# Every fourth chunk of the feed-forward weights: the remainder formed by an accumulating transfer instead of VectorE

## The chip, the cores and the metric

The kernel runs on one core of a Trainium2 chip. The metric is the device time of one execution, in microseconds, as the median of several runs; before the change it is 1503.18 us (three runs, 1502.87 to 1503.75).

## The reference, cut to what matters

One decoder layer over 256 tokens of width 2048, all in float32: a gated token mixer of two attention branches, a cross-attention into 256 memory tokens, and a SwiGLU feed-forward part. The change touches only the last:

```
def swiglu(x, w_in, w_out):
    g, u = jnp.split(x @ w_in, 2, axis=-1)
    return (jax.nn.silu(g) * u) @ w_out

    y = swiglu(x, w_ffn_in[l], w_ffn_out[l])
    x = layer_norm(ALPHA * x + y, ln_g[l, 2], ln_b[l, 2])
```

`w_ffn_in` is 2048 x 11264 (two halves of 5632 columns), `w_ffn_out` is 5632 x 2048.

## The kernel before

Every large product is [256 tokens, K] times streamed weights [K, 512]. TensorE takes float32 operands in its rounded form `F32R`, so each operand is split in two: hi is the value rounded to `F32R`, lo = value - hi is what the rounding leaves. A product then takes three matmuls for each block of 128 rows of K: hi x hi, hi x lo and lo x hi.

The weights come in chunks of 256 rows of K (two blocks, `KC = 2`) by 512 columns, 512 KB each. `chunk_in` (L193) brings one in:

- a load issued on SyncE's queue puts it into a tile `raw` (L204; pool of 5 buffers),
- ScalarE writes hi, the first half of a tile `hl`, by a copy that rounds (L116; pool of 4 buffers),
- VectorE writes lo = raw - hi into the second half (L117).

`chunk_mm` (L214) then issues six matmuls for each of the two groups of 128 tokens: L221 reads hi, L222 reads lo, L223 reads hi, twice over. That is 12 matmuls a chunk, into two accumulators of PSUM. `product` (L225) runs over the chunks. The feed-forward part (L816 on) has 11 column blocks of `w_ffn_in`, each with a gate product and an up product of 8 chunks, and then 4 column blocks of `w_ffn_out` with 22 chunks each. The first gate product and the last output product keep their last 8 chunks on chip (`seq=8`).

Nothing orders the engines but semaphores: a `hl` buffer is written again when the matmuls of the chunk four before have read it; a `raw` buffer is loaded again when its last reader is done; and SyncE's queue is in order, so a load that waits for its buffer holds back every transfer behind it. The order of the instructions on each engine is set when the kernel is built. Beside the chunks, SyncE also moves the finished blocks of the hidden activations out (`spill`, L190) and back in turned order (`turn`, L176).

Of the kernel before, what the change touches and what calls it, by code (L numbers as in the profile page):

```python
# [12 lines left out]
AF = mybir.ActivationFunctionType  # L13
ALU = mybir.AluOpType
# [14 lines left out]
DFF = 5632  # L29
# [8 lines left out]
KC = 2  # L38
NTURN = 2
W = 512  # L40


class Side:
    """Work that is emitted in small steps between the chunks of the main products."""

    def __init__(self):
        self.queue = []
# [18 lines left out]
def trunk(ctx: ExitStack, tc: tile.TileContext, a, out: bass.AP):  # L66
    nc = tc.nc
# [8 lines left out]
    last = [None]  # L76
    later = []
# [25 lines left out]
    def f(ap):  # L103
        return ap.bitcast(F32)

    class Quad:
        """Four blocks [128, 256] and what their rounding leaves, as operands of products."""

        def __init__(self, k=4, t=256):
            self.t = b8()  # L110
# [5 lines left out]
        nc.scalar.activation(hi, src, AF.Copy)  # L116
        (eng or nc.vector).tensor_tensor(lo, src, f(hi), op=ALU.subtract)  # L117

    # ---- constants
    ident = const.tile([P, P], F32, name="ident")  # L120
    make_identity(nc, ident)
    identr = const.tile([P, P], F32R, name="identr")
# [4 lines left out]
    for tt in range(NT):  # L127
        k = P * (tt + 1)
# [16 lines left out]
        return t  # L145

    def rstd(dst, var, scale):
        """(var * scale + eps) ** -0.5"""
        nc.gpsimd.tensor_scalar(dst, var, scale, EPS, op0=ALU.mult, op1=ALU.add)
        nc.gpsimd.tensor_tensor(dst, dst, mhalf, op=ALU.pow)  # L150

    # ---- transposes of [128 tokens, 512] into a quad
    def to_quad(q, tt, src):
        p = ps_aux()
        for i in range(4):
# [6 lines left out]
        to_quad(q, tt, src)  # L162
        yield

    # ---- the same for 256 tokens, from DRAM: the loads put columns 128 a .. 128 a + 127 into partitions
    # 32 a .. 32 a + 31, so that transposes of 32 by 32 are all that is left. Partition p of block k holds
    # column 4 p + k (mixed), or column 32 k + p % 32 of those (not mixed).
    def turn(q, src, mixed=True):
        q.mixed = mixed
        yield from turned(q.hi, q.lo, src, mixed)  # L170
# [18 lines left out]
    def keep(d, tt, src):  # L189
        nc.sync.dma_start(d[tt * P:(tt + 1) * P, :], src)  # L190

    # ---- products with streamed weights: [256 tokens, kts * 128] @ [kts * 128, n]
    def chunk_in(pieces, c, n, held=False, mixed=False, fine=None, eng=None):  # L193
        raw = stream.tile([P, KC, W], F32, tag="raw", name=nm("raw"), bufs=5)
        at = 0
        for w in pieces:
            m = w.shape[1]
            if mixed:
                g = c * KC // 4
                rows = w[g * W:(g + 1) * W, :].rearrange("(p k) n -> p k n", k=4)[:, c * KC % 4:c * KC % 4 + KC, :]  # L200
            else:
                rows = w[c * KC * P:(c + 1) * KC * P, :].rearrange("(k p) n -> p k n", p=P)
            for k in ([slice(i, i + 1) for i in range(KC)] if fine else [slice(0, KC)]):
                last[0] = nc.sync.dma_start(raw[:, k, at:at + m], rows[:, k, :])  # L204
                if fine:
                    next(fine, None)
            at += m
        t = b8() if held else stream.tile([P, D], F32R, tag="hl", name=nm("hl"), bufs=4)
        hi, lo = [t[:, i * KC * W:(i + 1) * KC * W].rearrange("p (k n) -> p k n", k=KC) for i in range(2)]
        for k in ([slice(i, i + 1) for i in range(KC)] if fine else [slice(0, KC)]):  # L210
            split(hi[:, k, :n], lo[:, k, :n], raw[:, k, :n], eng)
        return hi, lo
# [9 lines left out]
            nc.tensor.matmul(o[:, :n], xh, lo[:, kk, :n], start=False, stop=False)  # L222
            nc.tensor.matmul(o[:, :n], xl, hi[:, kk, :n], start=False, stop=k == kts - 1)  # L223

    def product(act, pieces, steps=1, before=None, first=None, seq=0, stream_seq=0, done=None):  # L225
        """act: quads; pieces: DRAM views of the weights' columns. The last seq chunks of weights stay on
        chip, and the first 128 tokens go through them before the others do."""
        n = sum(w.shape[1] for w in pieces)
        kts = pieces[0].shape[0] // P
        nchunk = kts // KC  # L230
        out = [ps_acc() for _ in range(NT)]
        for c in range(nchunk - seq):
            w = chunk_in(pieces, c, n, mixed=act[c * KC // 4].mixed, fine=first if c == 0 else None)
            if first is not None and c == 0:
                for _ in first:
                    pass
            if before is not None:
                before(c)
            for tt in range(NT):
                chunk_mm(out[tt], act, tt, c, kts, n, w)  # L240
            flush()
            side.step(steps)
        if seq:
            ws = []
            for i, c in enumerate(range(nchunk - seq, nchunk)):
                ws.append(chunk_in(pieces, c, n, held=i >= stream_seq, mixed=act[c * KC // 4].mixed, eng=nc.gpsimd if i % 4 == 2 else None))
                chunk_mm(out[0], act, 0, c, kts, n, ws[-1])
                side.step(steps)
            done(0, out[0])
            for i, c in enumerate(range(nchunk - seq, nchunk)):  # L250
                chunk_mm(out[1], act, 1, c, kts, n, ws[i])
                side.step(steps)
            done(1, out[1])
        elif done is not None:
            for tt in range(NT):
                done(tt, out[tt])
        return out
# [3 lines left out]
        nc.tensor.matmul(o, lh, rl, start=False, stop=False)  # L261
        nc.tensor.matmul(o, ll, rh, start=False, stop=stop)  # L262

    # ---- inputs
    x, mem = a["x"][0], a["mem"][0]
    w_in = a["w_in"][0]

# [15 lines left out]
    x0 = first_x()  # L283
    next(x0)

    # ---- the weights of the latents
    ukT, uv = [], []

    def latent_weights():
# [22 lines left out]
            uv.append(q)  # L312
            yield

    # ---- indexer queries: [hi; lo] of a head on the partitions
    qi = []
    for g in range(2):
        if g == 1:
# [3 lines left out]
        for tt in range(NT):  # L322
# [4 lines left out]
            for i in range(2):  # L327
                p = ps_aux(F32R)
# [4 lines left out]
                nc.scalar.activation(t[:, i * 4:i * 4 + 4, sl], pt, AF.Copy)  # L333
        qi.append(t)

    # ---- indexer keys, latents
    kvg = row_of(a["kv_norm_g"][0], LAT, "kvg")
    kig = row_of(a["idx_k_norm_g"][0], IDIM, "kig")
    kib = row_of(a["idx_k_norm_b"][0], IDIM, "kib")
# [7 lines left out]
    for tt in range(NT):  # L347
        sl = slice(tt * P, (tt + 1) * P)
        p = ps[tt]
# [29 lines left out]
            nc.tensor.transpose(pc[:, cc * P:(cc + 1) * P], ckv[tt].rearrange("p (c k) -> p k c", k=2)[:, cc], ident)  # L379
        split(ckT[:, 0, :, sl], ckT[:, 1, :, sl], pc[:, :2 * P].rearrange("p (c t) -> p c t", c=2))  # L380

    # ---- keys and values of the heads from the latents
    khT, vh = [], []

    def latent_heads():
# [43 lines left out]
            later.append(turn(q, d, False))  # L429
        return q  # L430

    # ---- attention of four heads
    def attention(q, kT, v, bias, slopes, oT, causal):
        width = 384 if causal else 512
        PT = [b8()[:, :4 * width].rearrange("p (h t) -> p h t", h=4) for _ in range(2)]
# [143 lines left out]
    side.finish()  # L579
    side.add(dsa())  # L580

    # ---- gate of the first branch, before its sigmoid
    ma = [b8(F32) for _ in range(NT)]
    for j in range(4):
        bias = bias_chunk(a["b_gate"][0][0, j * W:(j + 1) * W])
# [1 line left out]
        for tt in range(NT):  # L587
            nc.vector.tensor_tensor(ma[tt][:, j * W:(j + 1) * W], ps[tt], bias, op=ALU.add)

    # ---- block attention: one block, so causal over all keys  # L590
    oTb = [None, None]

    def moba(g, q, k, v):
# [10 lines left out]
    for g in range(2):  # L604
# [3 lines left out]
        side.add(moba(g, qm, km, vm))  # L608
        if g == 0:
            pass  # L610
    # the first branch must be done
    while oTa[1] is None or any(gen.__name__ == "dsa" for gen in side.queue):
        side.step(1)
    for tt in range(NT):
# [30 lines left out]
        q.mixed = True  # L645
        mT.append(q)

    # ---- residual and layer norm
    tok = []

    def load_row(dst, src):
# [10 lines left out]
            yield from load_row(tok[tt], x[tt * P:(tt + 1) * P, :])  # L662

    class Norm:
        """Residual sums and the layer norm over them."""

        def __init__(self, i):
            self.i = i
# [29 lines left out]
            eng.tensor_tensor(t, t, self.rows[1][:, cs], op=ALU.add)  # L698

        def run(self, tts, lag, far=()):  # L700
            """Blocks of 512 columns: norm, then transposes some steps later; those in far through DRAM."""
            if self.quads is None:
                self.quads = [Quad() for _ in range(4)]
            sc = {tt: self.scales(tt) for tt in tts}
            todo = [(tt, j) for j in range(4) for tt in tts]
            spills = {j: spill() for j in far}
            for i in range(len(todo) + lag):
                if i < len(todo):
                    tt, j = todo[i]
                    self.block(tt, j, sc[tt])  # L710
                    if j in far:
                        keep(spills[j], tt, tok[tt][:, j * W:(j + 1) * W])
                if i >= lag:
                    tt, j = todo[i - lag]
                    if j not in far:
                        to_quad(self.quads[j], tt, tok[tt][:, j * W:(j + 1) * W])
                    elif tt == tts[-1]:
                        for _ in turn(self.quads[j], spills[j]):
                            yield
                yield  # L720
# [46 lines left out]
            side.add(load_mem())  # L767
    side.finish()

    # ---- cross-attention  # L770
    w_kv = a["w_kv_mem"][0]
    side.add(n1.run(range(NT), 6, (2, 3)))
    side.step(2)
# [28 lines left out]
    for tt in range(NT):  # L802
        for j in range(4):
            p = ps_acc()
            kts = NMH * HD // P
# [6 lines left out]
        side.step(1)  # L812
    x2T = n2.quads

    # ---- feed-forward
    hT = []  # L816
    wf = a["w_ffn_in"][0]
    for j in range(DFF // W):
        gs = []

        def gate(tt, p):
            g = stage()
            nc.scalar.activation(g, p, AF.Silu)
            gs.append(g)

        if j == 0:
            product(x2T, [wf[:, j * W:(j + 1) * W]], seq=8, stream_seq=3, done=gate)
            side.finish()
        else:
            product(x2T, [wf[:, j * W:(j + 1) * W]], done=gate)  # L830
        pu = product(x2T, [wf[:, DFF + j * W:DFF + (j + 1) * W]])
        q = Quad()
        d = spill()
        for tt in range(NT):
            nc.vector.tensor_tensor(gs[tt], gs[tt], pu[tt], op=ALU.mult)
            keep(d, tt, gs[tt])
        later.append(turn(q, d))
        q.mixed = True
        hT.append(q)
    n3 = Norm(2)  # L840
    side.add(n3.load())
    for j in range(4):
        def finish(tt, p):
            n3.add(tt, j, p)
            if j == 3:
                n3.finish(tt)

        product(hT, [a["w_ffn_out"][0][:, j * W:(j + 1) * W]], seq=8 if j == 3 else 0, stream_seq=3, done=finish)


_INS = ["x", "mem", "w_in", "b_gate", "kv_norm_g", "idx_k_norm_g", "idx_k_norm_b", "w_uk", "w_uv", "w_o_dsa",
# [21 lines left out]
```

## Time and profile before

| what | value |
|---|---|
| median of three runs | 1503.18 us |
| span of the profiled execution | 1506.3 us, 3.1 us above the median |
| TensorE busy | 1464.6 us, 97% of the span |
| VectorE busy | 929.2 us, 62% |
| ScalarE busy | 684.2 us, 45% |
| GpSimd busy | 55.6 us, 4% |
| mean busy share of the 16 DMA engines on SyncE's queue | 69.7% |

No time of the profiled execution other than its span is given, so the span stands for it. How to read it: matmuls are pipelined, so a row of 0.39 us for one matmul overlaps the next; the distance between two starts is what one costs. An engine's busy share says nothing of who waits for whom; the rows that do are those of the waits, and those of the timeline, which give a start, a duration, and in brackets the idle time before it and what ended it.

### The profile page before, as it was taken

To read this page: it belongs to the slowest core of one execution; us is meant where nothing else is said; L and a number is where in the kernel's file an instruction comes from. 1 tells how busy PE (TensorE), PEld (TensorE's weight loads), DVE (VectorE), ACT (ScalarE), POOL (GpSimd) and SP (SyncE) were. 2 spreads that over 40 slices of the span, in tenths; PEclk is the share of its full clock that TensorE was granted. 3 is DMA by queue.
4 is the path that set the end of the run, shared out by engine and by line. 5 is a ranking of instruction groups with operands and counts; after the bars stand their busy time and mean duration, and the time that the engine had idled before them with its cause. 6 is when DMAs were issued, how large, how long until landed. Compare 5 with 4: busy or idle time off the path is not lost.

```text
span 1506.3 us, 17772 instructions
## 1 busy us (share of the span) xinstructions
PE 1464.6 (97%) x6640; PEld 1214.9 (81%) x6640; DVE 929.2 (62%) x1145; ACT 684.2 (45%) x798; POOL 55.6 (4%) x63
## 2 busy tenths in 40 slices
PE   7999999999999999889989999999999999999996
PEld 5988888888888887677878888888888888888885
DVE  6666986575756665776784555555455455545455
ACT  4645456454444443354753444444344444333342
POOL 0010000000000000040030000000000000000003
PEclk9999999999999999899999999999999999999998
DMA  9966667777667789749636667776777777666662
GB/s 272 235 181 185 193 207 233 220 251 224 206 200 224 230 257 281 192 141 298 204 117 201 208 210 222 222 220 204 231 217 204 223 219 248 193 200 190 194 218 88
DMA packets 201623, 318.71 MB, mean 212 GB/s; under 512 B 18880, under 2 KB 60992, under 8 KB 201536
## 3 DMA queue, kind: packets, MB, share of 16 engines
q1 hardware_dynamic: 201536, 317.57, 69.7%
q8 instruction: 52, 0.85, 0.2%
q14 instruction: 35, 0.29, 0.1%
HBM read 299.70 MB, written 17.83 MB: 211 GB/s over the span
## 4 chain that ended last, share of the span: by engine, by line
PE 51%; DVE 3%; DMA 1%; ACT 1%; issue 1%; POOL 0%; SPq 0%; ACTq 0%; DVEq 0%
PE acc L222 17%; PE acc L223 17%; PE acc L221 17%; DVE b L696 1%; DMA raw<-in_w_kv_mem 1%; DVE b L739 1%; PE aux L156 0%; ACT b L116 0%; DVE b L117 0%; DVE b L698 0%; DVE b L741 0%; DVE hl L117 0%; DVE lnst L681 0%; DVE b L680 0%; PE aux L261 0%
## 5 line engine op out<-in xcount | busy, mean ns | idle before, releaser
L117 DVE TENSOR_TENSOR hl<-raw,hl 128x1024 fp32r<-128x1024 f32 (+2 forms) x493 | 595.8, 1217 | 414.2 <-ACT hl L116 413.0
L116 ACT ACTIVATE hl<-raw 128x1024 fp32r<-128x1024 f32 (+2 forms) x495 | 516.2, 1051 | 592.4 <-PE acc L223 537.3
L222 PE MATMUL acc<-hl,b 128*128 128x512 f32 (+1 forms) x1976 | 771.8, 391 | 13.7 <-DVE hl L117 13.7
L221 PE MATMUL acc<-hl,b 128*128 128x512 f32 (+1 forms) x1976 | 769.5, 391 | 2.4 <-ACT b L182 1.7
L223 PE MATMUL acc<-hl,b 128*128 128x512 f32 (+1 forms) x1976 | 769.7, 390 | 1.1 <-DVE b L184 0.9
L222 PEld LDWEIGHTS acc<-hl,b 128*128 128x128 f32 x1976 | 373.3, 189 | 91.6 <-DVE hl L117 16.6
L221 PEld LDWEIGHTS acc<-hl,b 128*128 128x128 f32 x1976 | 373.3, 189 | 79.2 <-ACT b L182 2.5
L223 PEld LDWEIGHTS acc<-hl,b 128*128 128x128 f32 x1976 | 373.2, 189 | 78.8 <-DVE b L184 2.4
L181 DVE STREAM_TRANSPOSE tr<-turn 128x256 f32<-128x256 f32 (+1 forms) x156 | 71.3, 515 | 105.7 <-DMA turn<-spill 84.5
L182 ACT ACTIVATE b<-tr 128x1024 fp32r<-128x1024 f32 (+1 forms) x39 | 39.5, 1016 | 123.0 <-DVE tr L181 119.6
L184 DVE TENSOR_TENSOR b<-tr,b 128x1024 fp32r<-128x1024 f32 (+1 forms) x39 | 45.3, 1167 | 3.6 <-ACT b L182 3.0
L116 ACT ACTIVATE b<-aux 128x512 fp32r<-128x512 f32 (+1 forms) x44 | 23.2, 538 | 29.3 <-PE aux L262 15.5
L117 DVE TENSOR_TENSOR b<-aux,b 128x512 fp32r<-128x512 f32 (+1 forms) x44 | 26.1, 610 | 11.9 <-ACT b L116 11.7
L117 POOL TENSOR_TENSOR hl<-raw,hl 128x1024 fp32r<-128x1024 f32 x2 | 5.6, 2802 | 718.7 <-ACT hl L116 718.7
L222 PE MATMUL acc<-b,b 128*128 128x512 f32 x72 | 28.0, 391 | 0.3 <-DVE b L117 0.3
L221 PE MATMUL acc<-b,b 128*128 128x512 f32 x72 | 28.0, 393 | 0.1
L223 PE MATMUL acc<-b,b 128*128 128x512 f32 x72 | 27.9, 389 | 0.0
L117 DVE TENSOR_TENSOR b<-raw,b 128x1024 fp32r<-128x1024 f32 x16 | 23.1, 1461 | 7.7 <-ACT b L116 7.7
L261 PE MATMUL aux<-b,b 128*128 128x256 f32 (+1 forms) x80 | 21.9, 282 | 0.0
L116 ACT ACTIVATE b<-raw 128x1024 fp32r<-128x1024 f32 x18 | 18.4, 1059 | 5.9 <-DMA raw<-in_w_ffn_out 5.4
L262 PE MATMUL aux<-b,b 128*128 128x256 f32 (+1 forms) x80 | 21.0, 279 | 0.0
L260 PE MATMUL aux<-b,b 128*128 128x256 f32 (+1 forms) x80 | 20.8, 274 | 0.0
(129 smaller groups left out, 531.8 us busy)
## 6 DMA issues: line engine op xcount, KB each, us to landing
raw<-in_w_ffn_in SPq DMA_DIRECT2D x176, 512.0 KB, 4.5
raw<-in_w_in SPq DMA_DIRECT2D x143, 512.0 KB, 4.2
raw<-in_w_ffn_out SPq DMA_DIRECT2D x88, 512.0 KB, 4.2
raw<-in_w_out SPq DMA_DIRECT2D x32, 512.0 KB, 5.6
spill<-stage SPq DMA_DIRECT2D x56, 256.0 KB, 4.1
turn<-spill SPq DMA_DIRECT2D x112, 128.0 KB, 3.1
raw<-in_w_o_dsa SPq DMA_DIRECT2D x16, 512.0 KB, 4.5
raw<-in_w_o_moba SPq DMA_DIRECT2D x16, 512.0 KB, 4.2
```

The costliest lines, as they stand in the source:

```text
L116: nc.scalar.activation(hi, src, AF.Copy)
L117: (eng or nc.vector).tensor_tensor(lo, src, f(hi), op=ALU.subtract)
L181: nc.vector.transpose(tr[:, i, :], v[:, i])
L182: nc.scalar.activation(hi, tr, AF.Copy)
L184: nc.vector.tensor_tensor(lo, tr, f(hi), op=ALU.subtract)
L221: nc.tensor.matmul(o[:, :n], xh, hi[:, kk, :n], start=k == 0, stop=False)
L222: nc.tensor.matmul(o[:, :n], xh, lo[:, kk, :n], start=False, stop=False)
L223: nc.tensor.matmul(o[:, :n], xl, hi[:, kk, :n], start=False, stop=k == kts - 1)
L260: nc.tensor.matmul(o, lh, rh, start=start, stop=False)
L261: nc.tensor.matmul(o, lh, rl, start=False, stop=False)
L262: nc.tensor.matmul(o, ll, rh, start=False, stop=stop)
L696: nc.vector.tensor_tensor(t, t, self.rows[0][:, cs], op=ALU.mult)
```

## The change

`chunk_in` gets a flag `by_dma`. With it, the chunk's lo part is made in another way: ScalarE writes hi as before, then writes -hi into the lo half, and a transfer issued by GpSimd adds `raw` to the lo half where it lies. VectorE's subtraction is left out for that chunk. `product` gets `dma_every`: chunk c of a product takes the new way where c % 4 is 1. All the products of the feed-forward part get `dma_every=4`, but for the first gate product; chunks kept on chip (`seq`) stay as they were.

```
+        if by_dma:
+            nc.scalar.activation(hi, raw, AF.Copy)
+            nc.scalar.activation(lo, f(hi), AF.Copy, scale=-1.0)
+            nc.gpsimd.dma_start(f(lo), raw, accum_op=ALU.add)
+            return hi, lo
...
         for c in range(nchunk - seq):
-            w = chunk_in(pieces, c, n, mixed=act[c * KC // 4].mixed, fine=first if c == 0 else None)
+            w = chunk_in(pieces, c, n, mixed=act[c * KC // 4].mixed, fine=first if c == 0 else None,
+                         by_dma=dma_every and c % dma_every == 1)
...
-            product(x2T, [wf[:, j * W:(j + 1) * W]], done=gate)
-        pu = product(x2T, [wf[:, DFF + j * W:DFF + (j + 1) * W]])
+            product(x2T, [wf[:, j * W:(j + 1) * W]], done=gate, dma_every=4)
+        pu = product(x2T, [wf[:, DFF + j * W:DFF + (j + 1) * W]], dma_every=4)
...
-        product(hT, [a["w_ffn_out"][0][:, j * W:(j + 1) * W]], seq=8 if j == 3 else 0, stream_seq=3, done=finish)
+        product(hT, [a["w_ffn_out"][0][:, j * W:(j + 1) * W]], seq=8 if j == 3 else 0, stream_seq=3, done=finish, dma_every=4)
```

There are 64 such chunks: 42 in the 21 products over `w_ffn_in`, 18 in the first three over `w_ffn_out`, 4 in the last. ScalarE has 64 instructions more, VectorE 64 fewer, GpSimd 64 transfers more. Line numbers after L192 move by 4 to 7: L221 to L223 become L227 to L229.

The TensorE queue at such a chunk, the sixth of the first up product (its `hl` tile is hl_6418 before and hl_6419 after; acc_6329 and acc_6330 are the accumulators of the two token groups). Before:

```order
L221 MATMUL acc_6329<-hl_6418,b_907_6031 128x512 [waits Activation_49]
L222 MATMUL acc_6329<-hl_6418,b_907_6031 128x512 [waits DVE_49]
L223 MATMUL acc_6329<-hl_6418,b_907_6031 128x512
L221 MATMUL acc_6329<-hl_6418,b_907_6031 128x512
L222 MATMUL acc_6329<-hl_6418,b_907_6031 128x512
```

After:

```order
L227 MATMUL acc_6329<-hl_6419,b_907_6031 128x512 [waits Activation_49]
L227 MATMUL acc_6330<-hl_6419,b_907_6031 128x512
L228 MATMUL acc_6329<-hl_6419,b_907_6031 128x512 [waits DMASW1_49]
L229 MATMUL acc_6329<-hl_6419,b_907_6031 128x512
L227 MATMUL acc_6329<-hl_6419,b_907_6031 128x512
```

The first matmul that reads lo waits for the transfer (DMASW is GpSimd's transfers) instead of VectorE, and one matmul of the second token group that reads hi alone stands ahead of it now.

SyncE's queue around the load that takes the `raw` buffer of such a chunk (five loads after it). Before:

```order
L204 DMA raw_6416<-in_w_ffn_in 128x2x512 [waits DMAHW6_49,DVE_49]
L204 DMA raw_6433<-in_w_ffn_in 128x2x512 [waits DMAHW7_49,DVE_49]
L204 DMA raw_6450<-in_w_ffn_in 128x2x512 [waits DMAHW0_49,DVE_49]
L204 DMA raw_6475<-in_w_ffn_in 128x2x512 [waits DMAHW1_49,DVE_49]
L204 DMA raw_6497<-in_w_ffn_in 128x2x512 [waits DMAHW2_49,DVE_49]
```

After:

```order
L204 DMA raw_6417<-in_w_ffn_in 128x2x512 [waits DMAHW6_49,DVE_49]
L204 DMA raw_6435<-in_w_ffn_in 128x2x512 [waits DMAHW0_49,DVE_49]
L204 DMA raw_6452<-in_w_ffn_in 128x2x512 [waits DMAHW7_49,DMASW0_49]
L204 DMA raw_6477<-in_w_ffn_in 128x2x512 [waits DMAHW1_49,DVE_49]
L204 DMA raw_6499<-in_w_ffn_in 128x2x512 [waits DMAHW2_49,DVE_49]
```

One load in four waits for GpSimd's transfer where it waited for VectorE, and the loads behind it stand in the same queue.

ScalarE's queue at the same chunk, after (before, the second of these four rows is not there, and the first waits for DVE where this one has DMASW0):

```order
L212 ACTIVATE hl_6419<-raw_6417 128x1024 [waits DMASW0_49,DMAHW3_49,PE_49,Activation_49]
L213 ACTIVATE hl_6419<-hl_6419 128x1024 [waits Activation_49]
L116 ACTIVATE hl_6437<-raw_6435 128x1024 [waits DMAHW4_49,DVE_49,PE_49]
L116 ACTIVATE hl_6454<-raw_6452 128x1024 [waits DMAHW5_49,DVE_49,PE_49]
```

GpSimd's queue holds nothing but these 64 transfers from the first of them to the last. Apart from these, the `turn` transfers of a block stand one place later in SyncE's queue, and no other work has moved far.

## Rows read from the trace of the kernel before

**Rows 1.** The page's head: span, busy time and share of the busiest engines

```profile
span 1506.3 us, 17772 instructions
PE 1464.6 (97%) x6640; PEld 1214.9 (81%) x6640; DVE 929.2 (62%) x1145; ACT 684.2 (45%) x798; POOL 55.6 (4%) x63
```

**Rows 2.** Busy time by stretch: stretch, length, engines, granted clock, DMA share, GB/s

```profile
800.00:1240.00 440.00, 440.00 (x1943) 364.33 (x1942) 239.40 (x231) 189.56 (x191) 0.00 (x0) 1.00 0.71 216
1240.00:1470.00 230.00, 230.00 (x1016) 190.24 (x1014) 117.40 (x107) 92.41 (x89) 0.00 (x0) 1.00 0.66 207
```

**Rows 3.** Timeline of some chunks: start, us, engine, instruction, idle time before

```profile
1105.61 0.39 PE L223 MATMUL acc<-hl,b 128*128 128x512 f32 x1
1105.84 0.39 PE L221 MATMUL acc<-hl,b 128*128 128x512 f32 x1
...
1106.04 1.06 ACT L116 ACTIVATE hl<-raw 128x1024 fp32r<-128x1024 f32 x1 [1.66 <-PE acc L223]
1108.76 1.06 ACT L116 ACTIVATE hl<-raw 128x1024 fp32r<-128x1024 f32 x1 [1.66 <-PE acc L223]
...
1107.13 1.23 DVE L117 TENSOR_TENSOR hl<-raw,hl 128x1024 fp32r<-128x1024 f32 x1 [1.49 <-ACT hl L116]
...
1114.00 0.39 PE L221 MATMUL acc<-hl,b 128*128 128x512 f32 x1
1114.22 0.39 PE L222 MATMUL acc<-hl,b 128*128 128x512 f32 x1
1114.45 0.39 PE L223 MATMUL acc<-hl,b 128*128 128x512 f32 x1
```

**Rows 4.** Waits, 1000 to 1300 us: who for whom, total us, times, longest

```profile
ACT hl L116 <- PE acc L223: 139.3, 87, 1.7
DVE hl L117 <- ACT hl L116: 108.6, 82, 2.0
...
SPq L204 <- DVE hl L117: 206.1, 99, 5.7
```

**Rows 5.** Transfers, 1000 to 1300 us: queue's MB and share; issues, KB, us to landing

```profile
q1 hardware_dynamic: 39674, 66.00, 71.3%
...
raw<-in_w_ffn_in SPq DMA_DIRECT2D x87, 512.0 KB, 4.5
...
turn<-spill SPq DMA_DIRECT2D x25, 128.0 KB, 2.9
...
b<-in_ln_g SPq DMA_DIRECT2D x2, 512.0 KB, 8.3
```

**Rows 6.** The tile raw, 1100 to 1130 us: issue ns, and us to landing

```profile
L204 SPq DMA_DIRECT2D raw<-in_w_ffn_in x11: 367/368/398, 1100.2 to 1129.4; - x11
...
DMA to landing us min/median/max: 3.6/4.0/4.5
```

**Rows 7.** GpSimd's rows by line and shape, 600 to 1400 us: count, busy, mean ns

```profile
L150 POOL TENSOR_TENSOR lnr<-lnr,mhalf 128x1 f32<-128x1 f32 x4 | 3.2, 806 | 0.2
L117 POOL TENSOR_TENSOR hl<-raw,hl 128x1024 fp32r<-128x1024 f32 x1 | 3.1, 3103 | 28.3 <-ACT hl L116 28.3
```

**Rows 8.** Stretches with gaps on TensorE, columns as in rows 2

```profile
670.00:680.00 10.00, 6.24 (x18) 4.76 (x17) 10.00 (x9) 2.01 (x3) 5.17 (x3) 0.66 0.45 116
...
700.00:710.00 10.00, 9.09 (x40) 7.19 (x40) 6.66 (x9) 3.11 (x4) 0.00 (x0) 1.00 1.07 295
...
760.00:770.00 10.00, 7.92 (x36) 6.23 (x34) 9.75 (x15) 5.15 (x9) 3.69 (x4) 0.83 0.00 0
```

More of the change, by code (lines that the diff above doesn't have):

```diff
@@ L190, in keep, with chunk_in @@
         nc.sync.dma_start(d[tt * P:(tt + 1) * P, :], src)
-    def chunk_in(pieces, c, n, held=False, mixed=False, fine=None, eng=None):
+    def chunk_in(pieces, c, n, held=False, mixed=False, fine=None, eng=None, by_dma=False):
         raw = stream.tile([P, KC, W], F32, tag="raw", name=nm("raw"), bufs=5)
@@ L223, in chunk_mm, with product @@
             nc.tensor.matmul(o[:, :n], xl, hi[:, kk, :n], start=False, stop=k == kts - 1)
-    def product(act, pieces, steps=1, before=None, first=None, seq=0, stream_seq=0, done=None):
+    def product(act, pieces, steps=1, before=None, first=None, seq=0, stream_seq=0, done=None, dma_every=0):
         n = sum(w.shape[1] for w in pieces)
```

## The prediction

> **What bounds the kernel now.** The page's head comes first: TensorE is busy for 97% of the span, VectorE for 62%, GpSimd for 4% [rows 1]. Such shares are averages, so the table by stretch is next, for the feed-forward part alone: from 800 to 1240 us TensorE is busy 440.00 of 440.00 us, from 1240 to 1470 us 230.00 of 230.00, both at a granted clock of 1.00, the 2.4 GHz level [rows 2]. Nothing that another engine is relieved of can shorten these 670 us: TensorE does not wait there.
>
> The timeline then tells how far ahead the other engines are. Two starts of ScalarE's hi copy lie 1108.76 - 1106.04 = 2.72 us apart [rows 3], which is one chunk of 12 matmuls, 0.227 us each. ScalarE's copy starts when TensorE has finished the chunk that held the `hl` buffer: the matmul that starts at 1105.61 ends at 1106.00, the copy starts at 1106.04, after 1.66 us of waiting for TensorE [rows 3]. The waits say that this is the rule, 87 times in 300 us, as VectorE waits for ScalarE 82 times [rows 4]. So the split of a chunk begins as late as four buffers force it to, and TensorE then has the three chunks between in hand: it started the next one at 1105.84 and comes to the first matmul on the new buffer at 1105.84 + 3 x 2.72 = 1114.00, to the first that reads lo at 1114.22 [rows 3]. VectorE has lo ready at 1107.13 + 1.23 = 1108.36. It is 5.86 us early. **That lead is what the change spends**: it puts a longer chain into the place of a VectorE step that nobody waits for.
>
> **The change part by part.** *VectorE's 64 subtractions* go, 64 x 1.23 = 79 us of its busy time [rows 3]. On the path to the end they are worth nothing: TensorE's own work covers them, with 5.86 us to spare each.
>
> *ScalarE's 64 added copies* of -hi have the shape of the hi copy, 1.06 us [rows 3]. ScalarE is busy for 1.06 of 2.72 us a chunk; with one more in four chunks, 5 x 1.06 = 5.3 of 10.88 us. The next chunk's copy starts 2.72 us after this one, and the two copies take 2 x 1.06 + 0.03 = 2.15 us (0.03 being the handover seen from ScalarE at 1107.10 to VectorE at 1107.13). So nothing behind them in ScalarE's queue is held, and their cost is that the transfer starts later: -hi is there at 1106.04 + 2.15 = 1108.19.
>
> *The transfer's budget.* In the changed order one more matmul that reads hi stands ahead of the first that reads lo, so lo is wanted at 1114.00 + 2 x 0.227 = 1114.45. From 1108.19 that leaves 6.26 us for GpSimd's issue and for the transfer to land. Each microsecond over it is a TensorE stall. It comes back every four chunks: the buffer of the next such chunk is freed by TensorE only after the stalled one, so the stall is not made good in between.
>
> *GpSimd's issue.* No transfer issued by GpSimd is in this trace. From below, the same kind of command takes SyncE 0.37 us [rows 6]; from above, GpSimd's longest operation on a whole chunk takes 3.10 us [rows 7]. I take 0.8 us, its smallest two-input operation [rows 7], since what it must write is a list of 128 rows and not 128 x 1024 elements. Nothing else is on GpSimd's queue in the stretch (0.00 us busy [rows 2]), so nothing is held behind it.
>
> *The transfer itself.* It writes 512 KB and reads twice that, `raw` and lo. No accumulating transfer is in the trace either. From below: the quickest plain load of 512 KB lands 3.6 us after its issue [rows 6]; that is the price if the addition is free and its second read hidden. From above: the slowest 512 KB in the stretch takes 8.3 us [rows 5]. Between them: the usual load takes 4.5 us [rows 5], and a second read of 512 KB is one more 512 KB of engine time. 66.00 MB took 71.3% of 300 us, so 0.524 MB takes 0.713 x 300 / 126 = 1.70 us [rows 5]. I take 4.5 + 1.7 = 6.2 us, since what has to be moved is certain and that the reads are hidden is not.
>
> The Trainium skill, "DMA: Bandwidth & Descriptors", section "Anatomy of one DMA — SWDGE (gpsimd) path", gives such a transfer about 2.0 us plus its bytes over 436 GB/s; "Collectives: The Full Stack", section "The bandwidth ceiling: the fold count and why AG ≠ RS ≠ AR", says that an adding transfer is bound by its two source reads and not by the addition. By these two the estimate is 2.0 + 1.2 = 3.2 us for one read and 4.4 us for two, and the sum would be no stall at all; the rows here show 3.6 to 4.5 us already for one plain read.
>
> *The sum.* 0.8 + 6.2 = 7.0 us against 6.26: a stall of 0.74 us at each of 64 chunks, 47 us. From below, 0.37 + 3.6 = 4.0 us: no stall, and nothing gained. From above, 0.8 + 8.3 = 9.1 us: 2.84 us, 182 us; with both upper bounds at once, 11.4 us and 329 us. (Three of the 64 come two chunks after another and share part of its stall; that is under 3 us in the middle case.) The profiled execution's span is 3.1 us above the median [rows 1]; the additions are made to the median, 1503.2 us.
>
> *SyncE's queue.* A `raw` buffer now comes free when the transfer lands, at 1114.45 or later, instead of 1108.36, and the loads behind it wait too (SyncE waits for that release at nearly every load already, 99 times in 300 us [rows 4]). The load five chunks on then lands at 1114.45 + 4.5 = 1118.95; ScalarE wants it at 1106.04 + 5 x 2.72 = 1119.64. It fits by 0.7 us, with the 5.86 us of a normal chunk behind that. A stall shifts both sides alike. The same wait also keeps new loads off the DMA engines while the transfer runs, so I add nothing for contention. The `turn` and `spill` transfers behind have a whole product to land in.
>
> **The rivals.** *It fits (the other side: not slower).* The addition streams through at the price of a plain load: 0.8 + 3.6 to 4.5 = 4.4 to 5.3 us, under 6.26. For it: the transfer has little beside it on the queue, and the loads' 4.5 us are with other loads beside them. Against: the second read, and an issue by GpSimd that no row prices. Then TensorE stays at 100%, VectorE's relief is worth nothing, and the time is 1503.2 us. The point from which it decides is 6.26 us.
>
> *A slow transfer.* GpSimd needs microseconds to write its list, or the addition halves the engines' rate once more: 9.1 us or over, 1503 + 182 = 1685 us. Such gaps could also cost clock: in 10 us with 0.91 us of gap the granted clock stayed at 1.00, with 2.08 us it was 0.83, with 3.76 us 0.66 [rows 8]. But a slower TensorE also lengthens the three chunks in hand, so this rival limits itself.
>
> *The DMA engines are full.* Their share is 0.713 now, 7.76 us of four chunks' 10.88 [rows 5]. With two reads of 1.70 us more it is 11.16 us, 0.28 us too much: 64 x 0.28 = 18 us, 1521 us, as a rate and not as a latency. For it: the arithmetic; against: the loads reached 295 GB/s in one stretch [rows 8], above the 216 here [rows 2].
>
> *Faster.* TensorE has no wait left to remove in the stretch [rows 2], and the tail has none of the changed chunks. *That the change does not do what it says* is excluded by the order of the instructions: 64 transfers are there.
>
> **How the numbers follow.** Stall of about 0.74 us: 42%, its own range 0.1 to 2 us a chunk, 1510 to 1631 us. It fits: 36%. A slow transfer: 13%. Engines full: 6%. Faster for a reason not seen: 3%. The forecast is the likeliest, 1503 + 47 = 1550 us. The range runs from 1501, which holds the case that fits, to 1686, the upper bound with the middle issue; it leaves out the faster cases and about half of the slow ones, some 10%. A measurement of this kernel can tell about 0.2%, 3 us. Slower: 42 + 13 + 6 = 61%; same 36%; faster 3%.
>
> **What would show it.** In the changed kernel's profile: L228 waiting for a transfer into `hl`, 64 times; the time from the end of the -hi copy to the landing, 7.0 us, against a budget of 6.26; TensorE under 100% busy in the stretch, by 0.74 us in 11.6; every fourth ScalarE hi copy to hi copy distance longer by that. If there is no such wait, the forecast was wrong at the transfer's price, and the time is that of before. If the loads of `raw` are what ScalarE waits for, it was wrong at SyncE's queue. If the granted clock falls, the stall was mis-sized upward.

## The result and the profile after

The changed kernel takes 1578.61 us (median of four runs, 1573.25 to 1585.1) against 1503.47 for the kernel before beside it: a ratio of 1.0497, 95% interval 1.0471 to 1.0522. It is 75 us slower, about 1.2 us for each of the 64 transfers, as if each stalled a little. They don't: TensorE waits for 24 of them, 0.2 to 3.6 us each, and not at all for the other 40.

The page of the changed kernel, its head and its queues (packets, MB, share of 16 engines), and GpSimd's transfers (KB each, median us from issue to landing); they answer to [rows 1, 5]:

```profile
span 1577.7 us, 17971 instructions
...
PE 1489.1 (94%) x6640; PEld 1224.5 (78%) x6640; DVE 853.1 (54%) x1081; ACT 750.9 (48%) x862; POOL 110.5 (7%) x127
...
q1 hardware_dynamic: 201536, 317.57, 64.4%
q0 software_dynamic: 9216, 33.56, 12.1%
...
hl<-raw POOLq DMA_DIRECT2D x64, 512.0 KB, 5.3
```

The 64 transfers are the new queue q0. They hold the engines for 0.121 x 1577.7 / 64 = 2.98 us each, 1.75 times what a load of the same size took before (1.70 us). The table by stretch, with the columns of [rows 2]:

```profile
800.00:1240.00 440.00, 407.88 (x1730) 330.90 (x1728) 170.56 (x170) 205.04 (x207) 31.02 (x36) 0.97 0.85 234
1240.00:1540.00 300.00, 286.30 (x1227) 233.68 (x1227) 110.23 (x103) 141.25 (x135) 23.34 (x27) 0.98 0.85 242
```

TensorE was busy without a break in [rows 2]; now it idles for 32.1 and 13.7 us, and the granted clock is a little under 1. The waits of TensorE from 800 us on name one cause (us in total, times, longest):

```profile
PE acc L228 <- DMA hl<-raw: 45.8, 24, 3.6
```

So 24 of 64 transfers are late, not 64. The span grew by 71.4 us. The stalls make 45.8. The clock, 0.97 over 440 us and 0.98 over 300 us, makes some 13 + 6 = 19; that is an estimate from two rounded figures. The rest, some 6.5, fits the overlap that a stall breaks: the first matmul after it has a row of 0.50 us that overlaps nothing before it, where each of the others adds 0.227 (24 x 0.27).

Away from a block's end a cycle of four chunks looks like this (timeline, columns of [rows 3]):

```profile
1109.31 1.06 ACT L212 ACTIVATE hl<-raw 128x1024 fp32r<-128x1024 f32 x1 [1.71 <-PE acc L229]
1110.40 1.06 ACT L213 ACTIVATE hl<-hl 128x1024 fp32r<-128x1024 f32 x1
...
1120.19 1.06 ACT L212 ACTIVATE hl<-raw 128x1024 fp32r<-128x1024 f32 x1 [1.71 <-PE acc L229]
...
1111.82 0.86 POOL L214 DMA_DIRECT2D hl<-raw  x1 [10.05 <-ACT hl L213]
...
1117.22 0.62 PE L227 MATMUL acc<-hl,b 128*128 128x512 f32 x2
1117.67 0.39 PE L228 MATMUL acc<-hl,b 128*128 128x512 f32 x1
```

From one L212 to the next it is 10.88 us, four chunks of 2.72: no time is lost. -hi ends at 1111.46, GpSimd starts 0.36 us later, and lo is wanted at 1117.67, a budget of 6.21 us (6.26 was forecast). The transfer lands about 5 us after its start (from 1400 to 1480 us the median is 5.0), so it fits with 0.8 us to spare.

At a block's end it looks like this. SyncE moves the finished block out, and the turning loads wait for that; the two stalls of the block follow (ScalarE's rows, then TensorE's with their waits):

```profile
1117.35 0.82 SPq L190 DMA_DIRECT2D spill<-stage  x2
...
1122.63 1.88 SPq L176 DMA_DIRECT2D turn<-spill  x4
...
1122.69 0.86 POOL L214 DMA_DIRECT2D hl<-raw  x1 [10.02 <-ACT hl L213]
...
1133.65 1.06 ACT L182 ACTIVATE b<-tr 128x1024 fp32r<-128x1024 f32 x1 [7.02 <-DVE tr L181]
1134.62 1.05 ACT L116 ACTIVATE hl<-raw 128x1024 fp32r<-128x1024 f32 x1
1135.57 1.04 ACT L212 ACTIVATE hl<-raw 128x1024 fp32r<-128x1024 f32 x1
...
1130.04 0.50 PE L228 MATMUL acc<-hl,b 128*128 128x512 f32 x1 [1.33 <-DMA hl<-raw]
1144.27 0.50 PE L228 MATMUL acc<-hl,b 128*128 128x512 f32 x1 [3.04 <-DMA hl<-raw]
```

The first transfer starts with the turning loads and lands 7.3 us after its start, 1.33 us too late. The turning loads are slow as well: they land after 6.0 us (the median of the four), where the kernel before has 2.9 [rows 5]. ScalarE's next instruction in line is L182, the rounding copy of the turned block, and it waits 7.02 us for them while the copies of the next chunks, L212 and L213 among them, stand behind it. L212, due some 10.88 + 1.33 us after the one at 1120.19, so at 1132.4, starts at 1135.57. Its transfer starts at 1138.20, lands 6.0 us later, one more than away from a block's end, and TensorE waits 3.04 us. From 1145 to 1148 us the granted clock is 0.53, which is the 1.2 GHz level for most of the time:

```profile
1145.00:1148.00 3.00, 3.00 (x9) 2.27 (x9) 0.00 (x0) 0.00 (x0) 0.00 (x0) 0.53 0.92 295
```

Twenty of the 24 stalls are such pairs, from 833 to 1290 us. The other four are in the output product, and two of the longest are there, 3.64 us (1316.24) and 3.36 us (1515.05): both transfers start some 2.6 us after two loads of the last norm's rows (L662, 512 KB each) and land after 9.5 and 9.3 us.

The kernel before has the same wait of ScalarE, at L182 of a block's end, with nobody behind it that is in a hurry:

```profile
1134.24 1.06 ACT L182 ACTIVATE b<-tr 128x1024 fp32r<-128x1024 f32 x1 [2.66 <-DVE tr L181]
```

### The profile page after: what moved, and what is told of

Same layout as the page of the kernel before. It is cut to its first block, busy times and chain, and to the rows that moved or that the text cites. A ratio compares the mean times of both kernels' runs of the same rounds, so it can differ in the third digit from the quotient of the medians.

```text
span 1577.7 us, 17971 instructions
## 1 busy us (share of the span) xinstructions
PE 1489.1 (94%) x6640; PEld 1224.5 (78%) x6640; DVE 853.1 (54%) x1081; ACT 750.9 (48%) x862; POOL 110.5 (7%) x127
## 3 DMA queue, kind: packets, MB, share of 16 engines
q1 hardware_dynamic: 201536, 317.57, 64.4%
## 4 chain that ended last, share of the span: by engine, by line
PE 35%; DMA 15%; DVE 4%; ACT 3%; issue 1%; SPq 1%; POOL 0%; ACTq 0%; DVEq 0%; POOLq 0%
PE acc L228 12%; PE acc L229 11%; PE acc L227 11%; DMA hl<-raw 9%; DMA turn<-spill 2%; DMA spill<-stage 1%; ACT hl L213 1%; ACT hl L212 1%; DMA raw<-in_w_kv_mem 1%; DVE tr L181 1%; DVE hl L117 1%; DMA raw<-in_w_q_mem 1%; DVE b L703 1%; ACT hl L116 1%; DVE b L746 1%
## 5 line engine op out<-in xcount | busy, mean ns | idle before, releaser
L228 PE MATMUL acc<-hl,b 128*128 128x512 f32 (+1 forms) x1976 | 782.2, 396 | 59.6 <-DMA hl<-raw 45.8
L117 DVE TENSOR_TENSOR hl<-raw,hl 128x1024 fp32r<-128x1024 f32 (+2 forms) x429 | 518.3, 1216 | 522.6 <-ACT hl L116 521.7
L229 PE MATMUL acc<-hl,b 128*128 128x512 f32 (+1 forms) x1976 | 777.9, 394 | 1.0 <-DVE b L184 1.0
L227 PE MATMUL acc<-hl,b 128*128 128x512 f32 (+1 forms) x1976 | 762.7, 393 | 3.3 <-ACT b L182 2.6
L116 ACT ACTIVATE hl<-raw 128x1024 fp32r<-128x1024 f32 (+2 forms) x431 | 450.0, 1050 | 441.4 <-PE acc L229 385.1
L228 PEld LDWEIGHTS acc<-hl,b 128*128 128x128 f32 x1976 | 377.5, 191 | 150.6 <-DMA hl<-raw 56.9
L227 PEld LDWEIGHTS acc<-hl,b 128*128 128x128 f32 x1976 | 377.0, 191 | 82.0 <-ACT b L182 3.9
L229 PEld LDWEIGHTS acc<-hl,b 128*128 128x128 f32 x1976 | 377.6, 191 | 79.2 <-DVE b L184 2.3
L181 DVE STREAM_TRANSPOSE tr<-turn 128x256 f32<-128x256 f32 (+1 forms) x156 | 71.3, 515 | 138.4 <-DMA turn<-spill 119.0
L212 ACT ACTIVATE hl<-raw 128x1024 fp32r<-128x1024 f32 x64 | 67.7, 1058 | 145.1 <-PE acc L229 144.3
L182 ACT ACTIVATE b<-tr 128x1024 fp32r<-128x1024 f32 (+1 forms) x39 | 39.5, 1015 | 140.6 <-DVE tr L181 136.9
L214 POOL DMA_DIRECT2D hl<-raw x64 | 55.4, 866 | 696.8 <-ACT hl L213 589.6
L213 ACT ACTIVATE hl<-hl 128x1024 fp32r<-128x1024 f32 x64 | 67.9, 1061 | 2.0
L227 PE MATMUL acc<-b,b 128*128 128x512 f32 x72 | 28.0, 393 | 0.1
L229 PE MATMUL acc<-b,b 128*128 128x512 f32 x72 | 27.9, 390 | 0.0
L469 POOL TENSOR_SCALAR mx<-mx 128x4 f32<-128x4 f32 x10 | 4.0, 403 | 257.0 <-DVE mx L468 253.0
L268 PE MATMUL aux<-b,b 128*128 128x256 f32 (+1 forms) x80 | 21.8, 281 | 0.0
```

Source lines behind the costliest of these rows:

```text
L181: nc.vector.transpose(tr[:, i, :], v[:, i])
L182: nc.scalar.activation(hi, tr, AF.Copy)
L212: nc.scalar.activation(hi, raw, AF.Copy)
L213: nc.scalar.activation(lo, f(hi), AF.Copy, scale=-1.0)
L214: nc.gpsimd.dma_start(f(lo), raw, accum_op=ALU.add)
L227: nc.tensor.matmul(o[:, :n], xh, hi[:, kk, :n], start=k == 0, stop=False)
```

## The experiments

The theory after reading the trace: the transfer fits where nothing else is on the way, and is late only at a block's end, for two reasons. **Contention**: it shares the DMA engines with the turning loads. **ScalarE's held queue**: the -hi copy stands behind a copy that waits for those loads. The rivals: each transfer is over its budget (the forecast); the DMA engines have too much to move on average; ScalarE's added copies cost time.

Ratios are against the kernel before on the same chip, with 95% intervals.

| run | median us | ratio |
|---|---|---|
| the change | 1578.6 | 1.0497 [1.0471, 1.0522] |
| e1: no transfers | 1505.8 | 1.0006 [0.9990, 1.0022] |
| e4: no moves of the blocks | 1510.2 | 1.0035 [1.0008, 1.0062] |
| e7: late transposes | 1585.9 | 1.0553 [1.0526, 1.0580] |
| e8: chunks 3 and 7 | 1606.0 | 1.0680 [1.0653, 1.0706] |
| e3: five buffers | 1549.6 | 1.0296 [1.0253, 1.0338] |
| e11: L182 on VectorE | 1546.6 | 1.0246 [1.0201, 1.0291] |
| e12: chunk 5 alone | 1524.7 | 1.0118 [1.0084, 1.0153] |
| e13: chunk 1 alone | 1555.6 | 1.0326 [1.0291, 1.0361] |
| e14: chunk 1 alone, L182 on VectorE | 1515.8 | 1.0069 [1.0040, 1.0097] |
| e2: plain copy | 1526.3 | 1.0142 [1.0104, 1.0181] |
| e15: five buffers, L182 on VectorE | 1518.5 | 1.0094 [1.0063, 1.0125] |

### e1: the change without its transfers

```
-            nc.gpsimd.dma_start(f(lo), raw, accum_op=ALU.add)
```

> The changed kernel without its 64 transfers: ScalarE still writes hi and -hi, VectorE's 64 subtractions stay away, and lo is left as -hi (raw is not added). Theory 1 (the time is lost to transfers that land late at a block's end, where the hidden block is moved out and turned, and to ScalarE's queue that is held there): without the transfers nobody waits, 1503 to 1506 us. Theory 2 (the 64 added copies on ScalarE hold the hi copies behind them): 1510 us or more. If VectorE's relief were worth anything, it would show here as a time under 1500 us; I expect none.

The ratio is 1.0006, the interval holds 1. TensorE is busy for 669.67 of 670 us (columns of [rows 2]):

```profile
800.00:1470.00 670.00, 669.67 (x2955) 554.16 (x2954) 280.83 (x274) 350.54 (x344) 0.52 (x1) 1.00 0.70 214
```

ScalarE's 64 copies are hidden, and so was VectorE's work: with its 64 subtractions gone and nothing in their place the kernel is not faster. The change had nothing to win; all that it costs comes from the transfers.

### e4: the change without the moves of the hidden blocks

```
-        q = Quad()
-        d = spill()
+        q = Quad.__new__(Quad)
+        q.t, q.hi, q.lo, q.mixed = x2T[j % 4].t, x2T[j % 4].hi, x2T[j % 4].lo, True
         for tt in range(NT):
             nc.vector.tensor_tensor(gs[tt], gs[tt], pu[tt], op=ALU.mult)
-            keep(d, tt, gs[tt])
-        later.append(turn(q, d))
-        q.mixed = True
         hT.append(q)
```

> The changed kernel without the moves of the hidden blocks: the 11 finished blocks are not moved out and not turned back in, and the output product reads the normed input's quads in their place; all 64 accumulating transfers stay. Theory 1 (late only beside a block's end): the 20 or so stalls of the blocks go, a few may be left near the loads of the last norm's rows: 1503 to 1515 us. Theory 2 (each of the 64 transfers is over its budget by some 0.7 to 1.2 us, as forecast): about 1575 us. Theory 3 (the DMA engines have too much to move on average): a little better than 1578, 1550 to 1570 us, since the blocks' moves are under a tenth of the bytes.

All 64 transfers are there, and 0.35% is lost instead of 5%. The DMA engines are as busy as with the change, 0.86 against 0.85 (first row below, columns of [rows 2]). This settles that a transfer is not over its budget by itself, and that its average load on the DMA engines is not the matter. It takes both suspected causes away at once, so it does not tell them apart. TensorE's only waits for transfers are these four. The last three stand at the boundaries of the output product's column blocks, 61 us apart, where two such chunks follow at a distance of two; the first belongs to a transfer that starts at 1245.44 between loads of the last norm's rows (L662 at 1240.77 and 1248.23) and lands after 6.7 us:

```profile
800.00:1470.00 670.00, 666.21 (x2934) 549.97 (x2933) 244.74 (x217) 335.75 (x327) 53.67 (x63) 1.00 0.86 244
...
1252.20 0.50 PE L228 MATMUL acc<-hl,b 128*128 128x512 f32 x1 [0.88 <-DMA hl<-raw]
1313.31 0.50 PE L228 MATMUL acc<-hl,b 128*128 128x512 f32 x1 [0.96 <-DMA hl<-raw]
1374.49 0.50 PE L228 MATMUL acc<-hl,b 128*128 128x512 f32 x1 [1.04 <-DMA hl<-raw]
1435.43 0.50 PE L228 MATMUL acc<-hl,b 128*128 128x512 f32 x1 [0.80 <-DMA hl<-raw]
```

### e7 and e8: the transposes three chunks later; chunks 3 and 7 instead of 1 and 5

```
-        yield
+        for _ in range(1 + lag):
+            yield
         tr = work.tile([P, 4, S], F32, tag="tr", name=nm("tr"))[:, :, :n]
...
-        later.append(turn(q, d))
+        later.append(turn(q, d, lag=3))
```

In e8 `c % dma_every == 3` as well.

> The changed kernel with the transposes of a turned block, and ScalarE's copy of them, put three chunks later in the program; the loads that they wait for stay where they are. Theory 1 with two causes: the first stall at a block's end (some 1.3 us, the transfer beside the turning loads) stays, the second (some 3 us and the lower clock after it, because ScalarE's copy of the transposes holds the hi copies behind it until the turning loads land) goes: 10 blocks x about 4.7 us = 45 us off, 1530 to 1540 us. If only the DMA engines' contention made both stalls: 1570 to 1580 us. If ScalarE's held queue made both: 1505 to 1515 us.

> As the late transposes, and chunks 3 and 7 of a product take the new way instead of 1 and 5 (c % 4 is 3), so that no accumulating transfer starts with the turning loads. Theory 1: the transfers now start 5.4 us after those loads, the first stall goes too, unless the moving out of the block, which chunk 7's transfer now meets, takes its place: 1505 to 1530 us. If the stalls do not come from what a transfer meets on the DMA engines, no better than the late transposes alone: 1530 us or more.

e7 missed. The code was moved and the instruction was not: in the order as built, ScalarE's copy of the turned block stands where it stood, since that order is set when the kernel is built and does not follow the text. So e7 is nearly the change again, with both stalls at each block (934.92 us: 1.45 us; 950.61 us: 3.79 us). It is a little slower than the change, with six waits of 0.3 to 0.9 us for VectorE beside. It tells nothing of the two causes.

e8 ends where its second line put it, at 1530 us or more, but not for the reason given there. Its lines are numbered one higher: L183 is ScalarE's copy of the turned block, L213 and L214 write hi and -hi, L215 is the transfer, L229 the matmul that reads lo. One block:

```profile
925.60 1.81 SPq L176 DMA_DIRECT2D turn<-spill  x4
925.84 0.86 POOL L215 DMA_DIRECT2D hl<-raw  x1 [12.58 <-ACT hl L214]
931.88 0.50 PE L229 MATMUL acc<-hl,b 128*128 128x512 f32 x1 [2.55 <-DMA hl<-raw]
...
935.38 1.06 ACT L183 ACTIVATE b<-tr 128x1024 fp32r<-128x1024 f32 x1 [5.41 <-DVE tr L182]
936.34 1.05 ACT L213 ACTIVATE hl<-raw 128x1024 fp32r<-128x1024 f32 x1
938.84 0.86 POOL L215 DMA_DIRECT2D hl<-raw  x1 [12.14 <-PE acc L230]
...
952.59 0.86 POOL L215 DMA_DIRECT2D hl<-raw  x1 [12.89 <-PE acc L230]
959.32 0.50 PE L229 MATMUL acc<-hl,b 128*128 128x512 f32 x1 [3.76 <-DMA hl<-raw]
```

The transfers did not get away from the turning loads: the one at 925.84 starts 0.24 us after them, and it stalls TensorE. The one directly behind ScalarE's held copy, at 938.84, lands after 4.8 us, and nobody waits for it. The second stall belongs to the next transfer, which lands after 6.7 us and has no copy ahead of it that waits for the turning loads. Stalls of about 2.6 and 3.9 us come so at every block, 6.8% in all. The run moved the transfers into other waits and does not separate the causes either.

### e11: the rounding copy of a turned block on VectorE

```
-        nc.scalar.activation(hi, tr, AF.Copy)
+        if on_dve:
+            nc.vector.tensor_copy(hi, tr)
+        else:
+            nc.scalar.activation(hi, tr, AF.Copy)
```

> The changed kernel with the rounding copy of a turned feed-forward block on VectorE instead of ScalarE, so that ScalarE's queue no longer waits for the turning loads. (The run that put this copy later in the program did not move it: it stood at the same place in ScalarE's queue.) If ScalarE's held queue makes the second stall of a block (some 3 us, and the lower clock after it), that stall goes and the first stays: 1530 to 1540 us. If contention on the DMA engines makes both: 1570 to 1590 us.

ScalarE no longer waits for the turning loads, and half of the loss is gone, 5.0% to 2.5%. From 830 to 1250 us TensorE's waits for a transfer are now 0.3 to 0.8 us, but for one of 1.6, and the granted clock from 800 to 1240 us is 1.00 (0.97 with the change). So the first stall of a block, which was expected to stay at 1.3 us, has become shorter too; why is not shown. Three waits of 1.7 to 3.6 us are left in the output product. VectorE, which is held by the transposes as before and has the copy in addition, is waited for five times, 0.5 to 1.8 us, 4.6 us together. The time lies some 7 us over the expected 1530 to 1540, and these waits are part of it.

### e12 and e13: one such chunk a product, chunk 5 or chunk 1

```
-                         by_dma=dma_every and c % dma_every == 1)
+                         by_dma=dma_every and c % 8 == 5)
```

In e13 `c % 8 == 1`.

> Half as many accumulating transfers, those of the chunks with c % 8 = 5: the gate product's is the one that starts with the turning loads. Theory 1: the first stall of a block stays (about 1.3 us and 0.3 us to restart), the second has no transfer to hit: 1503 + 10 x 1.6 and a little, 1518 to 1528 us. If the stalls came evenly from the number of transfers: half of 75 us, about 1541 us.

> Half as many accumulating transfers, those of the chunks with c % 8 = 1: none starts with the turning loads, and the up product's is the one behind ScalarE's held copy. Theory 1: with no transfer beside them the turning loads land in about 3 us as before, ScalarE is held for as long as before and that is nearly covered: 1503 to 1515 us. If ScalarE's hold alone, with no help from the first stall, makes the second: 10 x about 4.7 us, some 1550 us. If the stalls came evenly from the number of transfers: about 1541 us.

Each takes half of the transfers. With chunk 5 alone the transfer beside the turning loads is left. It starts some 2.7 us after the first of them here, when most are about to land (3.3 us, the median from 830 to 1240 us), and the one at 1050.02 still takes 7.3 us: nine waits of 0.4 to 1.7 us and one of 3.7 us near the end, 1.2% in all, as expected. With chunk 1 alone no transfer is beside the turning loads; the one behind ScalarE's copy is left, and the cost is 3.3%. I had expected the turning loads to land in about 3 us and the hold to be harmless. Both were wrong: the loads take 4.9 us (median, 830 to 1240 us), though no transfer starts beside them, and the rival line of the same expectation, some 1550 us, is what came. ScalarE's queue in e13:

```profile
979.52 1.06 ACT L182 ACTIVATE b<-tr 128x1024 fp32r<-128x1024 f32 x1 [4.78 <-DVE tr L181]
980.49 1.05 ACT L116 ACTIVATE hl<-raw 128x1024 fp32r<-128x1024 f32 x1
981.44 1.04 ACT L212 ACTIVATE hl<-raw 128x1024 fp32r<-128x1024 f32 x1
982.51 1.06 ACT L213 ACTIVATE hl<-hl 128x1024 fp32r<-128x1024 f32 x1
...
983.93 0.87 POOL L214 DMA_DIRECT2D hl<-raw  x1 [23.18 <-ACT hl L213]
...
990.36 0.50 PE L228 MATMUL acc<-hl,b 128*128 128x512 f32 x1 [2.66 <-DMA hl<-raw]
```

With the copies at 2.72 us from one another, as they are until 973.68, the L212 at 981.44 would have begun at 979.12. The hold costs it 2.3 us, the transfer takes 6.4 us from its start where 5.0 is usual away from a block's end, and the 0.8 us to spare are gone: 2.3 + 1.4 - 0.8 = 2.9, where 2.66 was measured. So the 3.3% is not the hold's alone. Without the slower landing the stall would be about 1.5 us, and in seven blocks of e13, from 885 us on, this transfer takes 6.1 to 6.9 us. 1.2% and 3.3% add up to 4.4% of the change's 5.0%: the chunk behind the held copy costs more than the chunk beside the turning loads. How the cost divides between the hold and contention is not shown.

### e14: both causes away

Chunk 1 alone as in e13 and the copy on VectorE as in e11.

> Both causes away at once, with 32 transfers left: chunks with c % 8 = 1 alone, so that no transfer starts with the turning loads, and the turned block's copy on VectorE, so that ScalarE is not held. Theory 1: both stalls of a block go; 1503 to 1512 us. If a transfer is over its budget wherever it stands: 32 x 1.2 = 38 us, about 1541 us.

0.7% is left, a little above what was expected: five waits of TensorE for a transfer remain, 6.4 us together, three of them after 1190 us, where the longest is 3.07 us. That longest one, at 1263.12, waits for a transfer that starts at 1254.12, 2.6 us after two 512 KB loads of the last norm's rows (L665 in this kernel, at 1251.52), and lands after 9.0 us. It is the place of the change's 3.64 us stall, and a second place where a transfer meets others.

### e3 and e15: five buffers for hl

```
-        t = work.tile([P, W], F32, tag="bias", name=nm("bias"), bufs=3)
+        t = work.tile([P, W], F32, tag="bias", name=nm("bias"), bufs=1)
...
-        t = b8() if held else stream.tile([P, D], F32R, tag="hl", name=nm("hl"), bufs=4)
+        t = b8() if held else stream.tile([P, D], F32R, tag="hl", name=nm("hl"), bufs=5)
```

In e15 the copy stands on VectorE as in e11 besides.

> The changed kernel with five buffers for hl instead of four (the bias tile, which the feed-forward part does not use, has one buffer instead of three, to make room). The split of a chunk then begins one chunk, 2.72 us, earlier, so the transfer's budget is 6.26 + 2.72 = 8.98 us. Theory 1 (late only beside a block's end): the first stall of a block goes (its transfer landed 7.3 us after the issue), the second shrinks from some 3 us to under 1 us: 1503 to 1515 us. Theory 2 (a rate: the DMA engines cannot move it all): a deeper buffer does not help a rate, 1560 us or more.

> All 64 accumulating transfers, the turned block's copy on VectorE, and five buffers for hl (one for the bias tile): the second stall's cause away, and a budget 2.72 us longer, which the first (about 1.3 us) fits. Theory 1: 1503 to 1520 us, the least that 64 such transfers can be made to cost with these two means; not under 1503, since TensorE has no wait to give back.

e3 missed: 1549.6 us where 1503 to 1515 was expected. A longer lead moves ScalarE ahead, but only as far as L182, which waits for a load that does not come sooner. It now waits up to 10.9 us there, 8 times, 64.4 us together (830 to 1500 us):

```profile
ACT b L182 <- DVE tr L181: 64.4, 8, 10.9
```

With that copy out of the way the fifth buffer does its work: e15 has all 64 transfers and loses 0.9%, in waits of mostly under 0.7 us. It is the cheapest form of the full change that was run, and still slower than the kernel before.

### e2: the same transfers without the addition

```
-            nc.gpsimd.dma_start(f(lo), raw, accum_op=ALU.add)
+            nc.gpsimd.dma_start(f(lo), raw)
```

> The price of the addition: the 64 transfers copy raw over -hi and add nothing, so lo is raw and not raw - hi; everything else is the changed kernel. If the second read is what makes an accumulating transfer cost more, the share of the DMA engines per transfer falls from some 2.98 us to 1.7 us and its landing from 5.1 us to 3.6 to 4.2 us in the undisturbed stretch, the first stall of a block goes, and the second (ScalarE held) shrinks by about 1 us: 1535 to 1560 us. If the addition is free: the same times and the same 1578 us.

The queue of the 64 transfers and their landing between 900 and 1200 us:

```profile
q0 software_dynamic: 9216, 33.56, 5.9%
...
hl<-raw POOLq DMA_DIRECT2D x27, 512.0 KB, 4.0
```

A plain copy holds the engines for 0.059 x 1528.6 / 64 = 1.41 us, the accumulating one for 2.98: the addition doubles it, which is what a second read would do, though no row shows the reads themselves. It lands after 4.0 us instead of 5.1 in the same stretch. One microsecond a transfer takes the loss from 5.0% to 1.4%, more than was expected: away from a block's end the change has 0.8 us to spare, and a transfer that lands a microsecond sooner has 1.8. That this is the reason is argued, not shown.

## Why the prediction was right, and where not

The time, 1550 forecast and 1578.6 measured, came out on the right side and in the range, by a sum whose main term was wrong.

- *TensorE bounds, VectorE's relief is worth nothing*: right, and shown by e1.
- *ScalarE's added copies are hidden*: right by e1.
- *The budget*: 6.26 us forecast, 6.21 measured.
- *GpSimd's issue*: 0.8 us forecast. 0.36 us pass from -hi's end to the start of the 0.86 us that GpSimd is busy, and the 5.0 us to the landing run from that start. So issue and landing together take 5.4 us away from a block's end, not 7.0.
- *The transfer*: the second read was rightly counted (1.70 + 1.70 us of engine time forecast, 2.98 measured). The landing was put at 4.5 + 1.7 = 6.2 us and is 5.0 in the undisturbed stretch. Both parts were too dear: e2's plain copy lands after 4.0 us, and the addition makes it 1.1 longer, not 1.7. The rows had 3.6 to 4.0 us for a plain load [rows 6]. With 4.0 for 4.5 the sum would have been 6.5, still 0.2 over the budget; with 0.36 for the issue as well it is 6.1, and it fits. (The 8.3 us of the upper bound are a median of two loads, not the slowest.)
- *64 stalls of 0.74 us*: wrong. In the undisturbed stretch there are none; the rival "it fits" describes that stretch. There are 24 stalls of 1.9 us on average, 20 of them at the end of a hidden block.
- *Nothing added for contention*: wrong, and this step is what the forecast lacked. I argued that SyncE's held queue keeps new loads away while the transfer runs, and that the `turn` and `spill` transfers have a whole product to land in. The first is not what the trace shows: a transfer that starts at 1405.81 has a new weight load beside it from 1408.3 on. It does little harm, since transfers land after 5.0 us there and ScalarE waited for weight loads 1.0 us in all (830 to 1540 us). The second looked at the block's own use, and not at ScalarE's L182 and VectorE's L181, which wait for it in queues that the split of the chunks needs. The trace of before held this wait, from 1000 to 1300 us (us in total, times, longest):

```profile
ACT b L182 <- DVE tr L181: 21.5, 5, 6.0
```

  It was up to 6 us long, and TensorE did not idle [rows 2]: the lead of 5.86 us [rows 3] covered it. e1 has such waits too, up to 6.5 us, and loses nothing. The change spent that lead a second time.
- *SyncE's queue*: right; SyncE waited for transfers 56 times between 830 and 1500 us, and no hi copy into an `hl` buffer waited for a load.
- *The engines' capacity as a rival* (1521 us): not it, by e4, with the same transfers and a DMA share of 0.86, at 1510.
- *The clock*: the rows of before gave the right sign. Stalls of 3 us are followed by stretches at 1.2 GHz, some 19 us in all by the estimate above, and the sum had nothing for it.

That two errors of opposite sign, too dear a transfer and no collision, gave nearly the right sum is luck. Even the waits add up to 45.8 us where 47 was forecast. Only their count, 24 and not 64, and their place show that the mechanism was another one. The range, 1501 to 1686 us, would have held the case that fits as well.

## What to carry to other kernels

A lead that nobody seems to use may be what covers a wait elsewhere: before spending it, look for the longest wait of each engine whose queue the new chain goes through, not for its usual one. A step that is moved to a transfer should be priced at the place in the program where other transfers meet it, since the average stretch can be free and a block's end cost nearly everything. And moving work off an engine that nobody waits for has no gain to set against any of this; leaving the work out altogether, as e1 does, shows that in one run.

## What the runs showed of the hardware that was not expected

- An accumulating transfer of 512 KB within the on-chip memory, issued by GpSimd, keeps GpSimd busy for 0.86 us, holds the 16 engines for 2.98 us and lands after 4.8 to 5.3 us with weight loads alone beside it (e4, 1055 to 1080 us). The plain copy: 0.53 us (32.29 us of GpSimd for 61 instructions, e2), 1.41 us and 4.1 to 4.6 us in the same stretch.
- Where it starts with four turning loads of 128 KB (1122.63 us), the transfer takes 7.3 us and the loads 6.0; in the kernel before, with weight loads beside them, they take 2.9 [rows 5]. Which transfer slows which is not shown: in e13 they take 4.9 us with no such transfer beside them, in e12 3.3 with one that starts 2.7 us later.
- A stall of 1.3 us left the granted clock at 1.00 (1130 to 1134 us); after one of 3.0 us it was 0.53, nearly the 1.2 GHz level, from 1145 to 1148 us.
